# A hybrid decoder layer on one core: the copies into G turned, two diagonals, six row buffers, and the split of the transposed rows moved to the last groups of the G stage

## The chip, the core and the metric

The kernel runs on one core of one Trainium2 chip. The metric is the device time of one execution in microseconds (us). Several executions are timed, and their median is quoted. One execution was also profiled.

## The reference, cut to what matters

The layer works on 512 tokens of width 1024. A mixing sub-layer (sparse attention and a gated linear recurrence) ends in a layer norm. Behind it stands PEER, a retrieval over 128 x 128 = 16384 single-neuron experts:

```python
cand = s_top[:, :, 0, :, None] + s_top[:, :, 1, None, :]
cand_idx = i_top[:, :, 0, :, None] * 128 + i_top[:, :, 1, None, :]
best, pos = lax.top_k(cand.reshape(128, 8, 256), 16)
experts = jnp.take_along_axis(cand_idx.reshape(128, 8, 256), pos, axis=-1)
g = jax.nn.softmax(best, axis=-1)
h = jax.nn.gelu(jnp.einsum('td,thkd->thk', xb, u[experts]))
out = jnp.einsum('thk,thkd->td', g * h, v[experts])
```

Each token has 8 heads of 16 chosen experts, so 128 pairs (i, j), each with a gate weight. The last step is again a layer norm of ALPHA * h plus this sum.

## The kernel before

**Blocks.** The 512 tokens are four blocks of 128. Block 0 is mixed first, then blocks 1 to 3 together. For the retrieval, blocks 0 and 1 fetch the chosen rows of u and v by indirect DMA ("rows", one gather of 128 rows of 1024 numbers for each k of 128). Blocks 2 and 3 (`DENSE`) multiply with all 16384 experts instead, and a matrix G with the gate weight of every token at every expert picks the right ones.

**Rows.** `peer_gather` is a generator. Each step gathers rows on GpSimd's queue (L641) and lets VectorE work on them: the u rows are multiplied with the hidden state and summed (L665), the v rows are weighted and added (L678). Other code advances it by `pump`. Of block 0's v rows, the last 52 are not added by VectorE but by TensorE (`pe_gather`): ScalarE makes a diagonal `dg` from the identity and a gate column (L694), and TensorE multiplies it with the gathered rows (L696). The first 14 go to the tiles `pv` in the routing stage, 38 go to `pw`: `PEPRE` = 8 of them ahead of the G stage in the program, and 30 spread over its groups. There is one buffer for `dg`.

**Row buffers.** A gather writes in turn to four buffers of the pool tag `g` and to any buffer whose tag is in the list `lent`. Those are 128x1024 tiles that are not needed elsewhere for the moment. When the queries of blocks 1 to 3 are done, `lent` is cleared: `hx0`, `hx1`, `hs2` and `hs3` then take the transposed hidden state of blocks 2 and 3, split into a high part `hTh` (rounded, on ScalarE) and a low part `hTl` (the difference, on VectorE), 8 instructions in all (L893 and L894). From there to the end four buffers take rows.

**The G stage.** In `dense`, TensorE transposes indices and gates of blocks 2 and 3 (L725) and ScalarE copies them to `dtr` (L727). Then 64 groups of 4 tokens follow. For each, VectorE makes two one-hot tiles `og` of 128x512 (L749), and ScalarE multiplies the gate weight into the second of them, one token (128x128) an instruction (L753): 4 tokens in every other group, 3 in the rest, where VectorE does the fourth (L755). `GACTS` sets this. TensorE multiplies the two for each token (L758) into a PSUM tile `gb` of 4 x 128 (two buffers), and ScalarE copies that into G (L736, `evacuate`). G is laid out as expert row j, then token t, so the copy writes 128 numbers that lie 1024 bytes apart, for each of 4 tokens. In every third group the rows are pumped by one step.

**The dense stage.** For each of 128 j: hidden products with `hTh` and `hTl` (L785), GELU, weighting with `G[:, j, :]` (L791), and the sum into `acc` (L805). The rest of the rows of blocks 0 and 1 are pumped between.

**Order.** The Tile framework's scheduler orders each engine's instructions when the program is built, from a timing model of its own and the number of buffers of each tag. An engine then runs its list in order.

Of the kernel before, what the change touches and what calls it, by code (L numbers as in the profile page):

```python
# [9 lines left out]
F32 = mybir.dt.float32  # L10
F32R = mybir.dt.float32r
# [4 lines left out]
ALU = mybir.AluOpType  # L16
# [10 lines left out]
HGB = 5  # L27
GB = 4
UB = 4
VB = 3  # L30
HLB = 6
KB2 = 11
# [8 lines left out]
PEPRE = 8  # L41
PEG = 60

GACTS = (3, 4)

GPUMP = 3

# [4 lines left out]
def tile_decoder_layer(ctx, tc, a, out):  # L52
    nc = tc.nc

    cst = ctx.enter_context(tc.tile_pool(name="cst", bufs=1))
    gat = ctx.enter_context(tc.tile_pool(name="gat", bufs=5))
# [114 lines left out]
    hT_parts = {}  # L171
    lent = ["hs1", "hs2", "hs3", "hx0", "hx1"]
# [513 lines left out]
    def pe_gather(n, p):  # L686

        while 0 not in weighted:
            pump(1)
        ks = [pe_left.pop(0) for _ in range(n)]  # L690
        for k in ks:
            g = gather(a["v"], 0, k, "v")
            dg = gat.tile([128, 128], F32, name=f"dg{k}", tag="dg", bufs=1)
            nc.scalar.mul(dg, ident, gate[:, 0, k:k + 1])  # L694
            for i in range(2):
                nc.tensor.matmul(p[i], dg, g[:, i * 512:(i + 1) * 512], start=(k == ks[0]), stop=(k == ks[-1]))  # L696
            if k != ks[-1]:
                yield
        for i in range(2):
            y = hs[0][:, i * 512:(i + 1) * 512]  # L700
            nc.vector.tensor_tensor(y, y, p[i], op=ALU.add)
        yield
# [13 lines left out]
    def dense(den, dps):  # L716

        nb = len(DENSE)
        T = 128 * nb
        tr = {}  # L720
        hTh, hTl = hT_parts["h"], hT_parts["l"]
        for i, b in enumerate(DENSE):
            p = dps.tile([128, 512], F32, name=f"dtp{b}", tag="gb", bufs=2)
            for n, src in enumerate((keep[b][0], keep[b][1], gate[:, b, :])):
                nc.tensor.transpose(p[:, n * 128:(n + 1) * 128], src, ident)  # L725
            t = den.tile([128, 4, 128], F32, name=f"dtr{b}", tag="v", bufs=VB)
# [6 lines left out]
        G = den.tile([128, 128, T], F32, name="G")  # L733

        def evacuate(t0, p):
            nc.scalar.copy(G[:, :, t0:t0 + 4].rearrange("p j t -> p t j"), p)  # L736

        def pump_some(t0):
            if t0 // 4 % GPUMP == 0:
                pump(1)  # L740

        for t0 in range(0, T, 4):
            p = dps.tile([128, 4, 128], F32, name=f"gb{t0}", tag="gb", bufs=2)
            x = tr[DENSE[t0 // 128]]
            c = t0 % 128
            og = [den.tile([128, 4, 128], F32, name=f"og{t0}_{n}", tag=tag, bufs=bufs)
                  for n, (tag, bufs) in enumerate((("u", UB), ("hl", HLB)))]
            for n in range(2):
                nc.vector.tensor_tensor(og[n], iota[:, None, :].to_broadcast([128, 4, 128]),  # L749
                                        x[n][:, c:c + 4, None].to_broadcast([128, 4, 128]), op=ALU.is_equal)  # L750
            gact = GACTS[t0 // 4 % len(GACTS)]
            for tt in range(gact):
                nc.scalar.mul(og[1][:, tt, :], og[1][:, tt, :], x[2][:, c + tt:c + tt + 1])  # L753
            if gact < 4:
                nc.vector.tensor_tensor(og[1][:, gact:, :], og[1][:, gact:, :],  # L755
                                        x[2][:, c + gact:c + 4, None].to_broadcast([128, 4 - gact, 128]), op=ALU.mult)
            for tt in range(4):
                nc.tensor.matmul(p[:, tt, :], og[0][:, tt, :], og[1][:, tt, :], start=True, stop=True)  # L758
            if t0:
                evacuate(t0 - 4, last)  # L760
            last = p
            pump_some(t0)
            while pdone < PEK2 and pdone < PEPRE + (t0 // 4 + 1) * (PEK2 - PEPRE) // PEG:
                next(pw)
                pdone += 1
# [39 lines left out]
                    nc.tensor.matmul(acc[i][n], wt[:, sl], vt, start=(j == 0 and q == 0), stop=(j == 127 and q == 2))  # L805

        def residual():
            ia = gat.tile([128, 128], F32, name="ia", tag="dg", bufs=1)
            nc.scalar.mul(ia, ident, ALPHA)
            for i in range(nb):  # L810
                for n in range(2):
                    for c in range(4):
                        for t in (hTl, hTh):
                            nc.tensor.matmul(acc[i][n][:, c * 128:(c + 1) * 128],
                                             t[n].bitcast(F32)[:, c, i * 128:(i + 1) * 128], ia,
                                             start=False, stop=False)
# [29 lines left out]
    def stage(blocks, xT):  # L846
# [37 lines left out]
            for b in (1, 2):  # L884
                index["sc"][b] = choose(b, index["sc"][b])
        if blocks != [0]:
            lent.clear()
            for part, tags in (("h", ("hx0", "hx1")), ("l", ("hs2", "hs3"))):
                hT_parts[part] = [cst.tile([128, 4, 256], F32R, name=f"hT{part}{i}", tag=tag) for i, tag in enumerate(tags)]
            for k in range(0, 8, 2):  # L890
                x = hT[:, k:k + 2, 128:384]
                th, tl = [hT_parts[part][k // 4][:, k % 4:k % 4 + 2, :] for part in "hl"]
                nc.scalar.copy(th, x)  # L893
                nc.vector.tensor_tensor(tl, x, th.bitcast(F32), op=ALU.subtract)  # L894
            for _ in pe_gather(PEK1, [bank(f"pv{i}", "hg") for i in range(2)]):
                pass

# [57 lines left out]
```

## Time and profile before

| | |
|---|---|
| median of 3 runs | 1610.61 us (1610.09 to 1612.2) |
| profiled execution, its own time | 1619.35 us |
| its span, first to last instruction | 1617.6 us |
| TensorE busy | 1446.4 us, 89% of the span |
| VectorE busy | 1385.0 us, 86% |
| ScalarE busy | 707.1 us, 44% |
| GpSimd busy | 674.6 us, 42% |
| mean DMA rate | 289 GB/s |

The profile names TensorE PE (its weight loads PEld), VectorE DVE, ScalarE ACT, GpSimd POOL. Busy times are sums over stages that have different limits: the G stage and the dense stage follow one another, and ScalarE is busy in them to quite different degrees. The profiled execution is 8.7 us longer than the median of the timed runs, so a duration from the trace is a little on the long side for those.

### The profile page before, as it was taken

How to read it: one execution, taken by the hardware profiler on the slowest of the kernel's cores; microseconds unless marked ns; L12 is line 12 of the kernel's file. 1: busy time of each engine (PE TensorE's matmuls, PEld its weight loads, DVE VectorE, ACT ScalarE, POOL GpSimd, SP SyncE). 2: the span in 40 equal slices, each digit the busy share in tenths (PEclk: the TensorE clock that was granted, in tenths of full speed). 3: DMA queues.
4: the chain of work that ended last, by engine and by line, in shares of the span. 5: the costliest groups of instructions: out<-in, count | busy, mean ns of one | idle time of the engine just before them, and what ended most of it. 6: DMA issues, size and time to landing. Idle time of an engine off the chain costs nothing. (4 is left out here: it accounts for less than half of the span.)

```text
span 1617.6 us, 24516 instructions
## 1 busy us (share of the span) xinstructions
PE 1446.4 (89%) x7858; PEld 1090.0 (67%) x7858; DVE 1385.0 (86%) x3263; ACT 707.1 (44%) x1501; POOL 674.6 (42%) x531
## 2 busy tenths in 40 slices
PE   8997879755777799679989999999999999999996
PEld 4756534533443466236668888888888889989985
DVE  4219997888889889998887999899998999999998
ACT  3312121122332012249994555555555555555553
POOL 0000057757766440254443444444453346545440
PEclk9998989865789899999999999999999999999998
DMA  8454579989879871457678999999999999999995
GB/s 289 171 161 150 171 265 409 341 304 346 301 270 342 309 296 53 143 164 229 225 226 289 350 345 354 320 351 351 354 352 332 342 343 361 358 348 351 353 360 192
DMA packets 166162, 467.90 MB, mean 289 GB/s; under 512 B 18576, under 2 KB 18704, under 8 KB 165904
## 3 DMA queue, kind: packets, MB, share of 16 engines
q0 software_dynamic: 73728, 268.47, 47.4%
q1 hardware_dynamic: 92304, 197.86, 33.9%
q8 instruction: 62, 1.02, 0.2%
q14 instruction: 68, 0.56, 0.1%
HBM read 464.16 MB, written 2.10 MB: 288 GB/s over the span
## 5 line engine op out<-in xcount | busy, mean ns | idle before, releaser
L641 POOL DMA_INDIRECT gv<-in_v_dram,idx x256 | 340.8, 1331 | 400.4 <-DVE hs L678 237.5
L641 POOL DMA_INDIRECT gu<-in_u_dram,idx x256 | 323.0, 1262 | 433.3 <-DVE gu L665 193.0
L665 DVE SCALAR_TENSOR_TENSOR gu<-gu,hs 128x1024 f32<-128x1024 f32 x256 | 310.9, 1236 | 30.5 <-DMA gu<-in_u_dram,idx 30.0
L678 DVE SCALAR_TENSOR_TENSOR hs<-gv,gate,hs 128x1024 f32<-128x1024 f32 x204 | 261.5, 1282 | 12.1 <-DMA gv<-in_v_dram,idx 9.3
L774 ACT CAST v_0h<-v 128x512 fp32r<-128x512 f32 x128 | 79.7, 623 | 95.3 <-PE acc L805 57.9
L525 PE MATMUL pq<-hT,wpq 128*128 128x128 f32 (+1 forms) x512 | 118.4, 389 | 0.0
L774 ACT CAST v_1h<-v 128x512 fp32r<-128x512 f32 x128 | 79.5, 621 | 88.6 <-DMA v<-in_v_dram 40.2
L776 DVE TENSOR_TENSOR u_0l<-u,u_0h 128x512 fp32r<-128x512 f32 x128 | 88.5, 691 | 29.6 <-ACT u_0h L774 26.7
L774 ACT CAST u_0h<-u 128x512 fp32r<-128x512 f32 x128 | 79.3, 620 | 68.0 <-PE hp L785 32.1
L805 PE MATMUL acc<-v_0h,wl 128*128 128x512 f32 x256 | 102.0, 399 | 2.8 <-DVE wl L795 2.8
L776 DVE TENSOR_TENSOR v_1l<-v,v_1h 128x512 fp32r<-128x512 f32 x128 | 88.1, 688 | 17.2 <-ACT v_1h L774 13.9
L525 PEld LDWEIGHTS pq<-hT,wpq 128*128 128x128 f32 x512 | 79.9, 198 | 31.7 <-issue 1.1
L805 PE MATMUL acc<-v_0h,wh 128*128 128x512 f32 x256 | 101.2, 395 | 0.0
L774 ACT CAST u_1h<-u 128x512 fp32r<-128x512 f32 x128 | 79.4, 621 | 49.5 <-PE acc L805 42.1
L805 PE MATMUL acc<-v_1h,wl 128*128 128x512 f32 x256 | 100.3, 392 | 0.0
L805 PE MATMUL acc<-v_1h,wh 128*128 128x512 f32 x256 | 100.1, 391 | 0.0
L805 PE MATMUL acc<-v_0l,wh 128*128 128x512 f32 x256 | 99.7, 391 | 0.0
L776 DVE TENSOR_TENSOR u_1l<-u,u_1h 128x512 fp32r<-128x512 f32 x128 | 88.0, 687 | 5.8 <-ACT wh L793 2.3
L776 DVE TENSOR_TENSOR v_0l<-v,v_0h 128x512 fp32r<-128x512 f32 x128 | 88.2, 689 | 2.5 <-ACT v_0h L774 1.5
L785 PE MATMUL hp<-hTh,u_1l 128*128 128x256 f32 x512 | 84.8, 288 | 4.9 <-DVE u_1l L776 2.9
L785 PE MATMUL hp<-hTl,u_0h 128*128 128x256 f32 x512 | 83.8, 286 | 6.0 <-ACT u_0h L774 5.7
L785 PEld LDWEIGHTS hp<-hTl,u_0h 128*128 128x128 f32 x512 | 76.4, 189 | 18.6 <-ACT u_0h L774 8.8
(275 smaller groups left out, 3199.3 us busy)
## 6 DMA issues: line engine op xcount, KB each, us to landing
v<-in_v_dram SPq DMA_DIRECT2D x256, 256.0 KB
u<-in_ut_dram SPq DMA_DIRECT2D x256, 256.0 KB
wpq<-in_w_pq_dram SPq DMA_DIRECT2D x32, 512.0 KB
wo<-in_w_o_dram SPq DMA_DIRECT2D x16, 512.0 KB
hfw<-in_w_hf_dram SPq DMA_DIRECT2D x8, 512.0 KB
hqw<-in_w_hq_dram SPq DMA_DIRECT2D x8, 512.0 KB
hiw<-in_w_hi_dram SPq DMA_DIRECT2D x8, 512.0 KB
qaw<-in_w_qa_dram SPq DMA_DIRECT2D x8, 512.0 KB
```

Of the source, the lines that this page charges most:

```text
L525: nc.tensor.matmul(qp[:, :nt], w[:, k, :], hT[:, k, :nt], start=(k == 0), stop=(k == 7))
L641: nc.gpsimd.indirect_dma_start(out=t, out_offset=None, in_=table, in_offset=bass.IndirectOffsetOnAxis(ap=idx[b][k // 64][:, k % 64:k % 64 ...
L665: nc.vector.scalar_tensor_tensor(g, g, 1.0, hs[b], op0=ALU.mult, op1=ALU.mult, accum_out=hd[:, k:k + 1]))
L678: nc.vector.scalar_tensor_tensor(hs[b], g, gate[:, b, k:k + 1], hs[b], op0=ALU.mult, op1=ALU.add))
L774: nc.scalar.copy(h, x)
L776: nc.vector.tensor_tensor(l, x, h.bitcast(F32), op=ALU.subtract)
L785: nc.tensor.matmul(hp, ut[:, k * 128:(k + 1) * 128], ht[n][:, k, :], start=(n + q + k == 0), stop=(n == 1 and q == 2 and k == 3))
L805: nc.tensor.matmul(acc[i][n], wt[:, sl], vt, start=(j == 0 and q == 0), stop=(j == 127 and q == 2))
```

## The change

Four things are edited:

- **The copy into G is turned.** Source and target are walked in the other order: j outside, the 4 tokens inside. The writes now come in runs of 4 adjacent numbers (16 bytes), and the reads of PSUM jump 512 bytes from one number to the next.
- **`GACTS` is (4,)**: ScalarE does all four gate products in each group, VectorE none.
- **Two buffers for `dg`.**
- **`hs2` and `hs3` are lent to the rows**, so six buffers take rows from the routing stage on. In the place of the early split stand 4 plain copies to `hx0` and `hx1`. At group 56 (`t0 == T - 32`) the lending ends and the first half is split into `hs2` and `hs3`; at group 58 the second half is copied once more, into a row buffer of tag `g`, and split into `hx0` and `hx1`.

```diff
-GACTS = (3, 4)
+GACTS = (4,)
...
+DGB = 2
...
-            dg = gat.tile([128, 128], F32, name=f"dg{k}", tag="dg", bufs=1)
+            dg = gat.tile([128, 128], F32, name=f"dg{k}", tag="dg", bufs=DGB)
...
-            nc.scalar.copy(G[:, :, t0:t0 + 4].rearrange("p j t -> p t j"), p)
+            nc.scalar.copy(G[:, :, t0:t0 + 4], p.rearrange("p t j -> p j t"))
+
+        def split_hidden(x, h, l):
+            for k in (0, 2):
+                nc.scalar.copy(h[:, k:k + 2, :], x[:, k:k + 2, :])
+                nc.vector.tensor_tensor(l[:, k:k + 2, :], x[:, k:k + 2, :], h[:, k:k + 2, :].bitcast(F32), op=ALU.subtract)
...
+            if t0 == T - 32:
+                lent.clear()
+                x0, x1 = hT_parts["x"]
+                hTh, hTl = [[cst.tile([128, 4, 256], F32R, name=f"hT{part}0", tag=tag)]
+                            for part, tag in (("h", "hs2"), ("l", "hs3"))]
+                split_hidden(x0, hTh[0], hTl[0])
+            if t0 == T - 24:
+                x = gat.tile([128, 4, 256], F32, name="hTx1_moved", tag="g", bufs=GB)
+                nc.scalar.copy(x, x1)
+                for parts, part, tag in ((hTh, "h", "hx0"), (hTl, "l", "hx1")):
+                    parts.append(cst.tile([128, 4, 256], F32R, name=f"hT{part}1", tag=tag))
+                split_hidden(x, hTh[1], hTl[1])
...
-            lent.clear()
-            for part, tags in (("h", ("hx0", "hx1")), ("l", ("hs2", "hs3"))):
-                hT_parts[part] = [cst.tile([128, 4, 256], F32R, name=f"hT{part}{i}", tag=tag) for i, tag in enumerate(tags)]
+            lent[:] = ["hs2", "hs3"]
+            hT_parts["x"] = [cst.tile([128, 4, 256], F32, name=f"hTx{i}", tag=f"hx{i}") for i in range(2)]
             for k in range(0, 8, 2):
-                x = hT[:, k:k + 2, 128:384]
-                th, tl = [hT_parts[part][k // 4][:, k % 4:k % 4 + 2, :] for part in "hl"]
-                nc.scalar.copy(th, x)
-                nc.vector.tensor_tensor(tl, x, th.bitcast(F32), op=ALU.subtract)
+                nc.scalar.copy(hT_parts["x"][k // 4][:, k % 4:k % 4 + 2, :], hT[:, k:k + 2, 128:384])
```

The buffer counts also change the order that the scheduler makes. Three places follow, the kernel before first each time. The line numbers of the changed kernel are its own: its L697, L758 and L763 are L696, L753 and L758 before, and L736 is L736 in both.

On GpSimd's queue, where blocks 1 to 3 come out of their first layer norm, `gv_62` and so on are v rows of block 0 for VectorE, `gv_80` and `gv_81` are rows for the `pv` sums, which are due much later:

```order
210 L641 DMA gv_60_3460<-in_v_dram,idx_0_110 128x1024
211 L641 DMA gv_61_3463<-in_v_dram,idx_0_110 128x1024
212 L641 DMA gv_62_3466<-in_v_dram,idx_0_110 128x1024
213 L641 DMA gv_63_3485<-in_v_dram,idx_0_110 128x1024
214 L641 DMA gv_64_3488<-in_v_dram,idx_1_111 128x1024
```

```order
210 L642 DMA gv_60_3460<-in_v_dram,idx_0_110 128x1024
211 L642 DMA gv_61_3463<-in_v_dram,idx_0_110 128x1024
212 L642 DMA gv_80_4587<-in_v_dram,idx_1_111 128x1024
213 L642 DMA gv_81_4593<-in_v_dram,idx_1_111 128x1024
214 L642 DMA gv_62_3466<-in_v_dram,idx_0_110 128x1024
```

The two gathers that fill the newly lent `hs2` and `hs3` moved ahead of `gv_62`; they can start only when TensorE has transposed what those two buffers held.

On TensorE, at the end of routing: `dtp` are the transposes of indices (`ij`) and gates of the dense blocks, `pw` the products of the rows with a diagonal (`gv_90` is the first of them), `gb` the first groups of G:

```order
746 L725 MATMUL dtp_4669<-ident,ij_0_4114 128x128
747 L725 MATMUL dtp_4669<-ident,ij_1_4115 128x128
748 L725 MATMUL dtp_4669<-ident,gate 128x128
749 L696 MATMUL pw_4675<-gv_96_4713,dg_4715 128x512
750 L696 MATMUL pw_4676<-gv_96_4713,dg_4715 128x512
751 L696 MATMUL pw_4675<-gv_97_4719,dg_4721 128x512
752 L696 MATMUL pw_4676<-gv_97_4719,dg_4721 128x512
753 L758 MATMUL gb_4726<-og_1_4728,og_0_4727 128x128 x3
```

```order
750 L697 MATMUL pw_4669<-gv_98_4751,dg_4753 128x512
751 L697 MATMUL pw_4670<-gv_98_4751,dg_4753 128x512
752 L697 MATMUL pw_4669<-gv_99_4788,dg_4790 128x512
753 L697 MATMUL pw_4670<-gv_99_4788,dg_4790 128x512
754 L697 MATMUL pw_4669<-gv_100_4822,dg_4824 128x512
755 L697 MATMUL pw_4670<-gv_100_4822,dg_4824 128x512
756 L725 MATMUL dtp_4663<-ident,ij_0_4114 128x128
757 L725 MATMUL dtp_4663<-ident,ij_1_4115 128x128
758 L725 MATMUL dtp_4663<-ident,gate 128x128
759 L763 MATMUL gb_4720<-og_1_4722,og_0_4721 128x128 x4
```

The first `gb` stood behind 8 products of `pw` (`gv_90` to `gv_97`) and stands behind 11 now (to `gv_100`); all of these are ahead of the last transposes, where two followed them. On ScalarE, correspondingly, 13 of the 38 diagonals stand ahead of the copies to `dtr`, where 7 stood there before.

On ScalarE, near the end of the G stage of the changed kernel, the moved work among the groups (`hTx` is the kept copy, `hTh` the high part):

```order
440 L758 ACTIVATE og_1_5623<-og_1_5623,dtr_4667 128x128 x4
441 L758 ACTIVATE og_1_5637<-og_1_5637,dtr_4667 128x128 x4
442 L775 COPY hTx_moved<-hTx_4556 128x1024
443 L695 ACTIVATE dg_5810<-ident,gate 128x128
444 L736 COPY G<-gb_5550 128x128x4
445 L740 CAST hTh_5743<-hTx_4555 128x512 x2
446 L736 COPY G<-gb_5564 128x128x4
447 L758 ACTIVATE og_1_5660<-og_1_5660,dtr_4667 128x128 x4
448 L826 ACTIVATE ia<-ident 128x128
449 L758 ACTIVATE og_1_5674<-og_1_5674,dtr_4667 128x128 x4
450 L736 COPY G<-gb_5584 128x128x4
451 L740 CAST hTh_5788<-hTx_moved 128x512 x2
```

The copy to the row buffer and the two pairs of high parts are five instructions that ScalarE did not have in this stage before.

## Rows read from the trace of the kernel before

**Rows 1.** The page's first line.

```profile
span 1617.6 us, 24516 instructions
```

**Rows 2.** Windows: length, busy PE, PEld, DVE, ACT, POOL; clock, DMA share, GB/s.

```profile
590.00:620.00 30.00, 30.00 (x114) 19.10 (x113) 26.35 (x195) 5.81 (x12) 0.00 (x0) 1.00 0.41 143
620.00:655.00 35.00, 35.00 (x138) 22.42 (x137) 35.00 (x240) 10.98 (x19) 0.00 (x1) 1.00 0.03 10
655.00:713.00 58.00, 40.32 (x86) 14.38 (x84) 57.21 (x366) 15.50 (x33) 24.36 (x18) 0.94 0.51 155
713.50:849.00 135.50, 123.25 (x640) 84.01 (x638) 115.92 (x215) 130.36 (x322) 62.62 (x55) 0.99 0.71 228
849.00:1617.60 768.60, 741.48 (x4672) 666.50 (x4672) 701.87 (x1161) 399.44 (x775) 330.49 (x232) 0.99 0.94 337
```

**Rows 3.** Groups, 713 to 849 us: busy us, mean ns; idle us, releasers.

```profile
L749 DVE TENSOR_TENSOR og<-iota,dtr 128x512 f32<-128x512 f32 x128 | 81.1, 688 | 3.0 <-PE gb L758 2.2 <-ACT dtr L727 0.8
L753 ACT ACTIVATE og<-og,dtr 128x128 f32<-128x128 f32 x224 | 73.0, 412 | 0.0
...
L736 ACT COPY G<-gb 128x512 f32<-128x512 f32 x64 | 64.9, 1072 | 1.7 <-PE gb L758 1.7
...
L641 POOL DMA_INDIRECT gv<-in_v_dram,idx x31 | 37.9, 1223 | 25.3 <-PE pw L696 14.8 <-DVE gu L665 6.0 <-issue 3.0
...
L665 DVE SCALAR_TENSOR_TENSOR gu<-gu,hs 128x1024 f32<-128x1024 f32 x22 | 26.9, 1223 | 16.6 <-DMA gu<-in_u_dram,idx 16.6
...
L694 ACT ACTIVATE dg<-ident,gate 128x128 f32<-128x128 f32 x32 | 13.2, 412 | 5.5 <-PE pw L696 5.5
...
L755 DVE TENSOR_TENSOR og<-og,dtr 128x128 f32<-128x128 f32 x32 | 9.1, 285 | 0.2
```

**Rows 4.** ScalarE's timeline inside the G stage: start, length, instruction.

```profile
793.35 1.26 ACT L753 ACTIVATE og<-og,dtr 128x128 f32<-128x128 f32 x4
794.51 0.39 ACT L694 ACTIVATE dg<-ident,gate 128x128 f32<-128x128 f32 x1
...
795.68 1.94 ACT L736 COPY G<-gb 128x512 f32<-128x512 f32 x2
797.41 1.27 ACT L753 ACTIVATE og<-og,dtr 128x128 f32<-128x128 f32 x4
```

**Rows 5.** TensorE's timeline in the same stretch.

```profile
786.95 1.98 PE L696 MATMUL pw<-gv,dg 128*128 128x512 f32 x4 [0.33 <-ACT og L753]
788.77 2.00 PE L758 MATMUL gb<-og,og 128*128 128x128 f32 x16
790.95 1.98 PE L696 MATMUL pw<-gv,dg 128*128 128x512 f32 x4 [0.18 <-ACT dg L694]
```

**Rows 6.** ScalarE's timeline around the early split.

```profile
586.58 1.14 ACT L893 CAST hTh<-hT 128x512 fp32r<-128x512 f32 x2 [2.96 <-DVE hs L678]
...
590.40 1.57 ACT L534 COPY pss<-psc 128x512 f32<-128x512 f32 x3 [1.36 <-PE psc L529]
591.83 0.51 ACT L527 COPY pqs<-pq 128x384 f32<-128x384 f32 x1
```

**Rows 7.** VectorE's timeline at the same place.

```profile
587.74 2.49 DVE L894 TENSOR_TENSOR hTl<-hT,hTh 128x512 fp32r<-128x512 f32 x4
591.02 0.87 DVE L539 MAX8 sv<-pss 128x8 f32<-128x128 f32 x4 [0.79 <-ACT pss L534]
```

**Rows 8.** TensorE's timeline in the routing stage, the `pv` products.

```profile
657.75 1.98 PE L696 MATMUL pv<-gv,dg 128*128 128x512 f32 x4 [0.55 <-ACT dg L694]
660.29 1.98 PE L696 MATMUL pv<-gv,dg 128*128 128x512 f32 x4 [0.55 <-ACT dg L694]
...
687.45 3.77 PE L696 MATMUL pv<-gv,dg 128*128 128x512 f32 x4 [7.42 <-ACT dg L694]
```

**Rows 9.** All engines' timeline where `hs2` and `hs3` come free.

```profile
557.18 1.94 PE L213 MATMUL hT_ps<-ident,hs 128*128 128x128 f32 x8 [0.81 <-DVE hs L144]
...
558.50 1.86 POOL L641 DMA_INDIRECT gv<-in_v_dram,idx  x1 [14.04 <-DVE hs L678]
```

More of the change, by code (lines that the diff above doesn't have):

```diff
@@ L720, in dense @@
         tr = {}
-        hTh, hTl = hT_parts["h"], hT_parts["l"]
         for i, b in enumerate(DENSE):
@@ L807, in residual @@
         def residual():
-            ia = gat.tile([128, 128], F32, name="ia", tag="dg", bufs=1)
+            ia = gat.tile([128, 128], F32, name="ia", tag="dg", bufs=DGB)
             nc.scalar.mul(ia, ident, ALPHA)
```

## The prediction

> **What bounds the kernel now.** I read the stages first (busy time in windows), then the groups of the stage that the change touches, then its timeline engine by engine. In the windows [rows 2] the reader is to see three stages with three limits. From 590 to 655 us TensorE is busy all the time, and VectorE joins it at 620. From 655 to 713 VectorE is busy 57.2 of 58 us (routing), and TensorE only 40.3. Then comes the G stage, 713.5 to 849: ScalarE is busy 130.4 of 135.5 us, TensorE 123.3, VectorE 115.9. So ScalarE sets its pace, but TensorE stands only 7 us behind. Last comes the dense stage, 768.6 us, with TensorE at 741.5. No edit touches the work of that one: rows are pumped as often before it, and G has the same layout. The result is decided in the 135.5 us.
>
> The groups of the G stage [rows 3] show what fills ScalarE: 224 gate products, 64 copies into G, 32 diagonals. Their durations overlap, so I take what one occupies from the distance of starts in the timeline [rows 4]: four products from 793.35 to 794.51, 0.29 us each; a diagonal, of the same shape and the same mean of 412 ns [rows 3], as much; two copies into G from 795.68 to 797.41, 0.865 each. The check: 224 x 0.29 + 64 x 0.865 + 32 x 0.29 = 129.6, against 130.4 busy. TensorE in the same stretch [rows 5]: a product `pw` occupies 1.82 us (786.95 to 788.77), two groups of `gb` some 2.0, and its waits for ScalarE are only 0.2 to 0.3 us in a cycle of 4.0.
>
> **The change, part by part.**
>
> *The turned copy* is the large term, and no row shows it: nowhere in these rows does ScalarE read PSUM in jumps. Bounds: a copy of the same 512 numbers out of PSUM in plain order occupies 0.477 us (three from 590.40 to 591.83 [rows 6]); the present copy 0.865. I take 0.477, because the two differ only in the write order, and the new writes come in runs of four: 64 x 0.388 = 24.8 us less on ScalarE. The upper bound is no gain at all, 0.865.
>
> [...]
>
> *`GACTS` (4,)*: 32 more products on ScalarE, 32 x 0.29 = +9.3 us. VectorE loses 32 products of 0.285, at most 9.1 us [rows 3].
>
> *Diagonals and `pw`.* With two diagonals and six row buffers, the order puts 11 products `pw` ahead of the first group instead of 8, and 13 diagonals instead of 7 ahead of `dtr`. So the G stage loses 6 x 0.29 = 1.7 us on ScalarE and 3 x 1.82 = 5.5 us on TensorE. These products go to the routing stage. There a `pv` product starts every 2.53 us, 0.55 of it waiting for the single diagonal [rows 8]; with two it can be 1.98. From 655 to 713, 14 + 11 products take 25 x 1.98 = 49.5 us, and with the present wait of 7.42 for a gate column [rows 8] 56.9 of the 58 us. They just fit beside VectorE's work, which ends that stage; if they don't, the last transposes stand behind them on TensorE and G starts up to 2 us later. I count nothing for it.
>
> *The moved split.* In the G stage ScalarE gets four casts, 2 x 1.14 = 2.3 us, and one copy of 128x1024, priced as two of these, 1.1: +3.4 us. VectorE gets four subtractions, 2.5 us [rows 7]. Where they stood, four plain copies replace four casts on ScalarE (ScalarE is busy 5.8 of 30 us there [rows 2]), and VectorE loses 2.5 us at 588. I count that at nothing: VectorE then waits for TensorE's scores anyway (0.79 [rows 7], 3.65 us idle from 590 to 620), and TensorE is full until 655 [rows 2].
>
> *Six buffers on GpSimd's queue.* Two gathers into `hs2` and `hs3` now stand ahead of `gv_62`. They need the transposes that end at 559.1, while `gv_62` went out at 558.50 [rows 9]; each gather occupies the queue 1.2 us [rows 3], so what is behind it goes out 2 to 3 us later. VectorE's row additions then end that much later, and ScalarE's copies of the transposed rows wait for them (they wait 2.96 us now [rows 6]), with the `pss` copies behind them and VectorE's top-k behind these. The cover is the 2.5 us that VectorE no longer subtracts and its 3.65 idle until 620. So nothing; without the cover, 3 us. In the G stage six buffers let gathers go out earlier, and VectorE's wait of 16.6 us for u rows [rows 3] should shrink. Near its end the moved half holds one buffer; few gathers are left there.
>
> **The sum.** ScalarE: 130.4 - 24.8 + 9.3 - 1.7 + 3.4 = 116.6 us; with its present 5.1 idle, mostly at the start, 121.7. TensorE: 123.3 - 5.5 = 117.8; it can't lose its idle time at the start and at the end of the stage, some 5 us, so about 122.7. VectorE: 115.9 - 9.1 + 2.5 = 109.3 plus waits. Three engines then stand close together, TensorE and ScalarE handing two `gb` buffers to each other, so I add 1.3 us for waits that take turns: 124 us for the stage instead of 135.5, 11.5 us gained. The profiled execution took 1619.35 us, 1.75 more than its span of 1617.6 [rows 1], and would take 1607.9. It stands 8.7 us above the median of the runs, 1610.61, and I keep that distance: 1599.1 for the median.
>
> **The rivals.**
>
> *A: the price moves to the reading side (slower).* If the turned copy occupies 0.865 as before, ScalarE has 130.4 + 9.3 - 1.7 + 3.4 = 141.4 us, with 5.1 idle a stage of 146.5, 11 us longer: 1621.6. It decides at a copy of 0.693 us: 64 x 0.172 = 11.0 is what the other edits add to ScalarE. For it: no row has such a read, and the new pattern jumps 512 bytes at every number. Against it: the present copy, 0.865 against 0.477, reads in plain order and only writes in jumps, so the visible price is one of writing. One in five.
>
> *B: the rows become the bound.* ScalarE leaves the lead, but VectorE keeps its waits for u rows: 109.3 + 16.6 + 3.0 for groups and indices [rows 3] = 128.9 us, 6.6 gained, 1604.0. For it: TensorE and VectorE now take turns with GpSimd's single queue. Against it: six buffers. 15 in 100.
>
> *C: the edits cancel.* A copy between the bounds, about 0.69, gives ScalarE back just what the products and the split take from it, and the time stays within 0.2%. 8 in 100.
>
> **How the numbers follow.** The forecast has 55 in 100, rival B 15, C 8, A 20; 2 are left for a larger gain, up to the 18.9 us that a stage of ScalarE's 116.6 without idle time would give (1591.7). The forecast's own range is 1592 to 1606: from that lowest case to a stage that gains 4.6. The prediction is 1599.1. The range reaches from 1591 into the lower part of rival A, 1619; it leaves out most of A. A difference under 0.2% (3.2 us) is about what can't be told from no change here. Faster by more: forecast, B and the larger gain, 0.72. Within: C, 0.08. Slower: A, 0.20.
>
> **What would show it.** The row of the copy into G: near 0.6 us a piece (the plain copy's kind) in the forecast, near 1.07 in rival A. ScalarE in the G stage: no longer without any idle time, some 117 of 124 us, against 141 of 146. The number of `pw` products before the first `gb`: 11, and the first `og` still near 713; if it starts 2 us or more later, the cover in routing was too thin. VectorE's wait for u rows: under 5 us if the buffers help, 16 or more in rival B. The dense stage: 768 to 769 us as before; if that moves, the prediction is wrong in a place that it calls untouched.

## The result and the profile after

The changed kernel is slower: 1626.46 us, the median of 4 runs (1621.17 to 1627.2), against 1610.35 for the kernel before (1606.58 to 1612.2). The ratio is 1.0092, with a 95% interval of 1.0068 to 1.0115. The forecast was 1599.1 us, with a range of 1591 to 1619. Its profiled execution took 1627.2 us.

The page's first line and the windows of the changed kernel come first (length, busy PE, PEld, DVE, ACT, POOL; clock, DMA share, GB/s). The third window ends with VectorE's last index operation, the fourth with the first `og`, the fifth with the last `gb`.

```profile
span 1625.4 us, 24554 instructions
```

```profile
590.00:620.00 30.00, 30.00 (x118) 19.36 (x117) 29.96 (x231) 3.94 (x9) 0.00 (x0) 1.00 0.27 90
620.00:655.00 35.00, 35.00 (x126) 20.79 (x125) 35.00 (x219) 13.43 (x25) 6.52 (x5) 1.00 0.16 45
655.00:704.10 49.10, 30.72 (x69) 12.84 (x67) 49.03 (x324) 12.96 (x26) 25.18 (x14) 0.88 0.46 151
704.10:717.10 13.00, 7.93 (x15) 3.34 (x15) 0.03 (x1) 1.63 (x5) 6.60 (x8) 0.66 0.80 269
717.10:861.20 144.10, 120.85 (x630) 86.27 (x631) 113.31 (x195) 121.60 (x353) 51.22 (x48) 0.93 0.60 187
861.20:1625.40 764.20, 738.25 (x4665) 665.36 (x4663) 699.21 (x1153) 398.62 (x773) 328.39 (x230) 0.99 0.95 338
```

The reader is to see two things beside [rows 2]. For 13 us VectorE does nothing at all. And the G stage behind that is 144.1 us long, although no engine in it is full any more: ScalarE 121.6, TensorE 120.9, VectorE 113.3. The dense stage has not moved. The groups of the G stage (busy us, mean ns; idle us before, and releasers) say who waits:

```profile
L754 DVE TENSOR_TENSOR og<-iota,dtr 128x512 f32<-128x512 f32 x128 | 80.3, 684 | 41.2 <-PE gb L763 28.1 <-ACT dtr L727 13.0
...
L697 PE MATMUL pw<-gv,dg 128*128 128x512 f32 x120 | 64.4, 677 | 23.0 <-DMA gv<-in_v_dram,idx 22.3 <-ACT dg L695 0.6
...
L736 ACT COPY G<-gb 128x512 f32<-128x512 f32 x64 | 36.4, 577 | 10.5 <-PE gb L763 10.2
L666 DVE SCALAR_TENSOR_TENSOR gu<-gu,hs 128x1024 f32<-128x1024 f32 x23 | 28.0, 1216 | 0.0
```

Against [rows 3], the turned copy has a mean of 577 ns where it had 1072, and VectorE no longer waits for rows of u. In exchange TensorE waits 22.3 us for gathered rows of v, which stand in its list ahead of `gb`, and VectorE waits for TensorE and for `dtr`. One of TensorE's waits, 10.35 us, ends before the first `og` (below); from the first `og` to the last `gb` the table of waits (total us, times, longest) has

```profile
PE pw L697 <- DMA gv<-in_v_dram,idx: 12.0, 9, 2.9
```

**Where the time went.** I count from VectorE's last index operation, since executions differ ahead of it whatever the edit. The first transposes of `hT_ps` start at 552.70 us in the profile of before, and at 542.97 in that of the turned copy alone (below), though every engine's list is the same in both; after the change they start at 545.98, and over all kernels below between 542.97 and 559.67. From there to the last index it is 159.8 us before and 157.9 after, so that the edits cost nothing up to there. The last index comes at 712.49 before and at 703.90 after. From there to the first `hp` of the dense stage it is 137.1 us before (849.54) and 153.0 after (856.93): 16.0 us more, and the medians differ by 16.1. Of these, 12.2 are the later start (a wait of 13.00 for `dtr` in place of 0.76) and 9.6 the pace inside G (144.1 us from the first `og` to the last `gb`, 134.5 before); 5.8 come back at the end of G, where the first `hp` now stands 4.3 us ahead of the last `gb` and stood 1.5 behind it.

The start, in four timelines of the changed kernel (start, length, instruction, idle time before it): GpSimd, VectorE, TensorE, ScalarE.

```profile
691.18 1.36 POOL L642 DMA_INDIRECT gu<-in_u_dram,idx  x1 [0.30 <-PE pw L697]
692.84 11.60 POOL L642 DMA_INDIRECT gv<-in_v_dram,idx  x1 [0.30 <-PE pw L697]
704.74 0.94 POOL L642 DMA_INDIRECT gu<-in_u_dram,idx  x1 [0.30 <-issue]
```

```profile
703.90 0.22 DVE L623 SCALAR_TENSOR_TENSOR idx<-dc_v,dc_v 128x64 uint32<-128x64 f32 x1
717.12 1.29 DVE L754 TENSOR_TENSOR og<-iota,dtr 128x512 f32<-128x512 f32 x2 [13.00 <-ACT dtr L727]
```

```profile
683.91 12.26 PE L697 MATMUL pw<-gv,dg 128*128 128x512 f32 x28 [2.14 <-ACT gate L627]
...
708.57 7.60 PE L697 MATMUL pw<-gv,dg 128*128 128x512 f32 x12 [10.35 <-DMA gv<-in_v_dram,idx]
716.01 0.38 PE L725 MATMUL dtp<-ident,ij 128*128 128x128 f32 x2
```

```profile
716.27 0.40 ACT L695 ACTIVATE dg<-ident,gate 128x128 f32<-128x128 f32 x1 [1.31 <-PE pw L697]
716.58 0.84 ACT L727 COPY dtr<-dtp 128x384 f32<-128x384 f32 x2
...
734.45 1.04 ACT L736 COPY G<-gb 128x512 f32<-128x512 f32 x2
```

A gather that occupies GpSimd 0.94 us right behind it occupies it 11.60 here, until 0.3 us after VectorE's routing is done. TensorE's next `pw` product needs that row, and waits 10.35 us, to 4.1 us behind the gather's end. It is the first of three (a product is four matmuls), and the last transposes stand behind those, at 716.01. VectorE can't start G without them. (The last row, two copies into G, is for later.)

### The profile page after: what moved, and what is told of

The parts are those of the page before. It is cut to its first block, busy times and chain, and to the rows that moved or that the text cites. A ratio compares the mean times of both kernels' runs of the same rounds, so it can differ in the third digit from the quotient of the medians.

```text
span 1625.4 us, 24554 instructions
## 1 busy us (share of the span) xinstructions
PE 1444.4 (89%) x7858; PEld 1094.3 (67%) x7858; DVE 1376.8 (85%) x3231; ACT 699.1 (43%) x1538; POOL 681.6 (42%) x531
## 5 line engine op out<-in xcount | busy, mean ns | idle before, releaser
L642 POOL DMA_INDIRECT gv<-in_v_dram,idx x256 | 344.3, 1345 | 406.5 <-DVE hs L679 224.8
L642 POOL DMA_INDIRECT gu<-in_u_dram,idx x256 | 326.7, 1276 | 426.9 <-DVE gu L666 210.5
L754 DVE TENSOR_TENSOR og<-iota,dtr 128x512 f32<-128x512 f32 x128 | 80.3, 684 | 41.2 <-PE gb L763 28.1
L697 PE MATMUL pw<-gv,dg 128*128 128x512 f32 x152 | 78.5, 660 | 25.2 <-DMA gv<-in_v_dram,idx 22.3
```

Source lines behind the costliest of these rows:

```text
L642: nc.gpsimd.indirect_dma_start(out=t, out_offset=None, in_=table, in_offset=bass.IndirectOffsetOnAxis(ap=idx[b][k // 64][:, k % 64:k % 64 ...
```

## The experiments

The main theory was that the pieces work as forecast and the order around them loses the time: 11 products stand ahead of the last transposes, on rows that come late, and the gathers of v stand out of order on GpSimd. The rivals: an edit costs the time by itself (the turned read, the fourth product), or the six buffers do.

All ratios are to the kernel before on the same chip, with a 95% interval; 0.1% is 1.6 us. "G" is the profile's time from the start of the last index operation to the end of the last `gb`.

| kernel | `dg` buffers | row buffers | products on ScalarE | order kept | `pw` ahead | G, us | ratio (interval) |
|---|---|---|---|---|---|---|---|
| before (copy not turned) | 1 | 4 | 3, 4 | | 6 | 135.5 | 1 |
| changed | 2 | 6 | 4 | | 11 | 157.3 | 1.0092 (1.0068 to 1.0115) |
| turned copy alone | 1 | 4 | 3, 4 | | 6 | 131.1 | 0.9972 (0.995 to 0.9995) |
| with four products | 1 | 4 | 4 | | 6 | 144.0 | 1.0048 (1.0023 to 1.0072) |
| changed, one diagonal | 1 | 6 | 4 | | 3 | 137.7 | 1.0049 (1.0018 to 1.008) |
| changed, four rows | 2 | 4 | 4 | | 11 | 155.1 | 1.0146 (1.0093 to 1.0198) |
| products pinned | 2 | 6 | 4 | PE | 8 | 128.9 | 0.9963 (0.9943 to 0.9982) |
| gathers in order | 2 | 6 | 4 | POOL | 10 | 142.6 | 1.0032 (1.0011 to 1.0052) |
| both | 2 | 6 | 4 | PE, POOL | 8 | 124.9 | 0.9955 (0.9933 to 0.9978) |
| turned copy, six rows | 1 | 6 | 3, 4 | | 3 | 138.4 | 1.001 (0.9989 to 1.0032) |
| pinned, four rows | 2 | 4 | 4 | PE | 8 | 134.6 | 1.0011 (0.9981 to 1.004) |
| both, one diagonal | 1 | 6 | 4 | PE, POOL | 8 | 142.1 | 1.0081 (1.006 to 1.0103) |
| both, three and four products | 2 | 6 | 3, 4 | PE, POOL | 8 | 125.7 | 0.9953 (0.9928 to 0.9978) |
| four products, `og` pinned | 1 | 4 | 4 | DVE | 6 | 130.5 | 0.9958 (0.9937 to 0.998) |
| the same, u rows placed | 1 | 4 | 4 | DVE | 6 | 140.4 | 1.0026 (0.9997 to 1.0055) |

"`pw` ahead" counts the products ahead of the last transposes in TensorE's program order.

### The pieces one by one

**The turned copy alone.**

```diff
-            nc.scalar.copy(G[:, :, t0:t0 + 4].rearrange("p j t -> p t j"), p)
+            nc.scalar.copy(G[:, :, t0:t0 + 4], p.rearrange("p t j -> p j t"))
```

> The kernel before with the turned copy alone. Main theory (the 0.58 us copies seen after the change are a true gain, and the change loses elsewhere, at the late start of G and in its gathers): the order before G is that of the kernel before, 6 products of pw stand ahead of the last transposes, so VectorE's wait between routing and the first og stays under 2 us; ScalarE's busy time in G falls from 131 to about 103 us; G is then held by TensorE (120 us) and VectorE, and the time falls by 6 to 12 us, to 1598 to 1604 us. Rival 1 (the read at jumps of 512 bytes costs ScalarE or TensorE something that the copy's own row does not show): no gain, 1609 us or more.

0.9972: some 4.5 us faster, a little under the low end of what was expected. Every engine's list is that of before. The groups of its G stage:

```profile
L753 ACT ACTIVATE og<-og,dtr 128x128 f32<-128x128 f32 x224 | 72.1, 392 | 15.4 <-DVE og L749 15.4
...
L736 ACT COPY G<-gb 128x512 f32<-128x512 f32 x64 | 34.9, 571 | 2.1 <-PE gb L758 2.1
```

The copy is cheap, and ScalarE now waits 15.4 us for VectorE. VectorE in turn waits 14.6 us for rows of u, where it waited 16.6 [rows 3]. So the edit's own gain is real, rival A (and this study's rival 1) is out, and without ScalarE in the lead the rows hold the stage.

**Four products as well** (`GACTS` is (4,), nothing else).

> The turned copy and all four products on ScalarE, with four row buffers, one diagonal and the early split. Main theory: within 3 us of the run with the turned copy alone, VectorE's part of G shorter by about 9 us of busy time and ScalarE's longer by 9; 1597 to 1604 us. Rival 1 (the pieces themselves cost the time): 1612 us or more.

1.0048: 0.76% above the turned copy alone, some 12 us, where I had expected none. VectorE lost 9 us of work and the stage became 13 us longer. VectorE's wait for rows of u, in the table of waits (total us, times, longest), went from the first of these lines in the turned copy alone

```profile
DVE gu L665 <- DMA gu<-in_u_dram,idx: 14.6, 14, 3.0
```

to this one with four products:

```profile
DVE gu L665 <- DMA gu<-in_u_dram,idx: 29.5, 17, 3.3
```

TensorE's and GpSimd's lists are the same in both but for the first products in G. On VectorE the list changed: the rows of u stand behind groups 5, 5, 8, 10, 14, 16, 20, 22 in the one, and 1, 5, 8, 10, 12, 15, 19, 22 in the other. Two kernels further down take this up.

**The changed kernel with one diagonal** (`DGB` = 1) **and with four row buffers** (and the early split).

> The changed kernel with one diagonal instead of two; six row buffers and the late split stay. 3 products of pw now stand ahead of the last transposes instead of 11. Main theory: the wait for dtr between routing and G's first og falls from 13.0 us to under 2 us, and the time by 9 to 12 us, to 1614 to 1618 us; what stays above the turned copy alone is the pace of the gathers within G. Rival 2 (the six buffers, their order on GpSimd's queue, are the whole loss): it stays at 1623 to 1628 us with whatever wait.

> The turned copy, four products and two diagonals, with four row buffers and the early split. 11 products of pw stand ahead of the last transposes, as in the changed kernel, and the gathers stand in program order. Main theory: the first og comes 8 to 13 us after VectorE's last index operation, and the time is 8 to 12 us above the same kernel with one diagonal, 1607 to 1614 us. Rival 2 (the six buffers are the whole loss): within 2 us of the same kernel with one diagonal, 1597 to 1604 us.

With one diagonal the wait for `dtr` fell to 0.60 us, as expected, and the kernel is 0.43% faster than the changed one (the intervals overlap), 7 us of the 9 to 12 expected. G is 137.7 us; what it wins over the changed kernel it gives back in part behind G, where the span goes on for 778.6 us instead of 764.2. With four rows the late start is there with another set of buffers: 7.72 us of wait for `dtr`, and 0.98% (some 16 us, 8 to 12 expected) above the four-row kernel with one diagonal. So rival 2 is out: it is the two diagonals that bring the late start. The kernel lost more than that. In TensorE's list of before, one product stands behind every second group of G. In both kernels with two diagonals they stand unevenly (in the changed one in bunches, behind groups 8, 8, 10, 15, 15, 17, 21, 21, 23, 23, 25, 30, 30, in the four-row one behind 9, 9, 11, 13, 14, 17, 20, 21, 23, 26), and while TensorE waits for their rows the next groups wait behind them.

### The order put right

**The products pinned.** The 8 products are written ahead of the transposes, and TensorE keeps the order written:

```diff
-                nc.tensor.matmul(p[i], dg, g[:, i * 512:(i + 1) * 512], start=(k == ks[0]), stop=(k == ks[-1]))
+                tc.keep_in_program_order(
+                    nc.tensor.matmul(p[i], dg, g[:, i * 512:(i + 1) * 512], start=(k == ks[0]), stop=(k == ks[-1])))
...
+        pw = pe_gather(PEK2, [dps.tile([128, 512], F32, name=f"pw{n}", tag=f"acc0_{n}") for n in range(2)])
+        for _ in range(PEPRE):
+            next(pw)
+        pdone = PEPRE
...
-                nc.tensor.transpose(p[:, n * 128:(n + 1) * 128], src, ident)
+                tc.keep_in_program_order(nc.tensor.transpose(p[:, n * 128:(n + 1) * 128], src, ident))
```

> The changed kernel with 8 products of pw written ahead of the transposes, and the products and transposes of this stage kept in the order written on TensorE: 8 ahead of the last transposes instead of 11, then two products behind every second group of G. Main theory (G starts late since its transposes stand behind products that wait for a slow gather, and the four-row kernel with two diagonals lost 12 us so): VectorE's wait for dtr falls from 13.0 us to under 3 us and the time by 8 to 12 us, to 1614 to 1618 us. Rival (the fourth product on ScalarE is the loss, as 13 us between the two kernels with one diagonal and four rows would have it, and the start only moves the wait): the wait goes, the time stays above 1621 us.

0.9963, against 1.0092: 1.29% or some 21 us less than the changed kernel, twice what was expected, and all its edits are still in it. Its timelines of GpSimd and VectorE:

```profile
693.22 11.53 POOL L642 DMA_INDIRECT gv<-in_v_dram,idx  x1 [0.30 <-issue]
```

```profile
705.17 1.29 DVE L755 TENSOR_TENSOR og<-iota,dtr 128x512 f32<-128x512 f32 x2 [0.72 <-ACT dtr L732]
```

The slow gather is still there and as slow. But the product that needs it now stands behind the transposes, and nothing waits for it: 0.72 us for `dtr`. This settles the start, 12.3 us of the 21. The rest came inside G, where one product now stands behind every second group and TensorE waits for no row: it is 128.0 us from the first `og` to the last `gb`, 16 less than 144.1. Some 9 of these go again at its end, where the first `hp` stands 5.0 us behind the last `gb`.

**The gathers in order, and both together.** All row gathers are kept in program order on GpSimd; alone, and with the pinned products.

```diff
-        nc.gpsimd.indirect_dma_start(out=t, out_offset=None, in_=table,
-                                     in_offset=bass.IndirectOffsetOnAxis(ap=idx[b][k // 64][:, k % 64:k % 64 + 1], axis=0))
+        rows_in = nc.gpsimd.indirect_dma_start(
+            out=t, out_offset=None, in_=table,
+            in_offset=bass.IndirectOffsetOnAxis(ap=idx[b][k // 64][:, k % 64:k % 64 + 1], axis=0))
+        tc.keep_in_program_order(rows_in)
```

> The changed kernel with all row gathers kept on GpSimd's queue in the order in which the rows are used; 10 products of pw still stand ahead of the last transposes. Main theory: TensorE's wait for gathered rows within G (22 us in the changed kernel) falls under 10 us, the late start stays (5 us or more between the last index and the first og), and the time falls by 3 to 6 us, to 1620 to 1623 us. Rival (the order of the gathers is the whole loss): 1612 us or less.

> Both: 8 products pinned ahead of the transposes and the gathers in the order of use, with two diagonals, six row buffers, four products on ScalarE and the late split. Main theory: wait for dtr under 3 us, TensorE's wait for gathered rows in G under 8 us, G below 130 us from the first og, and 1600 to 1610 us. Rival (the fourth product on ScalarE is the loss): 1614 us or more, with VectorE waiting for rows of u.

Alone: 0.6% below the changed kernel, some 10 us, more than expected; 9.10 us of wait for `dtr` stay, and TensorE still waits 16.2 us for gathered rows from the last index on. Of these 7.8 are within G, where the changed kernel has 12.0; the 22 us of the expectation counted the wait at the start as well. Both: 0.9955, 1606.5 us against 1615.08 of the kernel before on that chip. The window from its first `og` to its last `gb`, and two of its groups:

```profile
706.60:830.70 124.10, 117.31 (x632) 81.00 (x632) 108.73 (x179) 117.98 (x354) 56.70 (x52) 0.97 0.70 230
```

```profile
L700 PE MATMUL pw<-gv,dg 128*128 128x512 f32 x120 | 57.5, 603 | 0.0
...
L739 ACT COPY G<-gb 128x512 f32<-128x512 f32 x64 | 35.2, 585 | 2.4 <-PE gb L766 2.4
```

TensorE waits for no row and no diagonal at all. A stage of the 124 us that the prediction worked out is here: 124.1 (134.5 before), with ScalarE at 118.0 (116.6 worked out), TensorE at 117.3 (117.8), VectorE at 108.7 (109.3). Whether the gathers' order adds to the pinned products can't be told: the intervals of 0.9963 and 0.9955 overlap, though G is 4 us shorter in the profile.

**The same with other buffers and products**, to see what each edit is worth where the order is even.

> The four-row kernel (turned copy, four products on ScalarE, two diagonals, early split) with 8 products pinned ahead of the transposes and two behind every second group, as in the pinned kernels with six rows; the gathers stand in the order of use. If the uneven order on TensorE was the loss there: the wait for dtr falls from 7.7 us to under 2 us and the time by 15 to 20 us, to about that of the kernel before plus or minus 4 us. What the pinned kernel with six rows has below it (it stood 0.45 per cent below the kernel before) is what the two rows more are worth: 3 to 10 us if VectorE's wait for rows of u (29.5 us with four rows and four products) is what they shorten, 0 if the rows were hidden.

> The kernel with pinned products and ordered gathers, with one diagonal instead of two. If two diagonals shorten TensorE's wait for dg (7 us in the kernel before, with one): 3 to 7 us slower than with two, with 5 us or more of PE waiting for dg. If the diagonal was hidden: within 2 us.

> The kernel with pinned products and ordered gathers, with three and four products on ScalarE in turn, as before the change. If the fourth product costs the time wherever it stands (13 us between the two kernels with four rows and one diagonal): 8 us or more faster than with four products. If that loss came from the order around it: within 3 us either way.

Pinned, the four-row kernel falls from 1.0146 to 1.0011, some 22 us, and its wait for `dtr` from 7.72 to 0.72 us: the order was its loss too. Six rows instead of four (and the late split with them) are worth 0.5% here (1.0011 against 0.9963 and 0.9955), some 8 us, as expected; VectorE waits 25.3 us for rows with four and 14.2 with six and the gathers in order. The fourth product makes no difference that can be told (0.9953 and 0.9955). The second diagonal is worth 1.3%, some 20 us, much more than expected. Inside G it is what was expected: with one diagonal TensorE waits 7.0 us for `dg`, and the stage is 129.9 us for 124.1 from the first `og` on. The larger part comes ahead of G. TensorE's timeline with one:

```profile
720.85 1.98 PE L700 MATMUL pw<-gv,dg 128*128 128x512 f32 x4 [0.55 <-ACT dg L697]
723.39 1.98 PE L700 MATMUL pw<-gv,dg 128*128 128x512 f32 x4 [0.55 <-ACT dg L697]
725.92 1.98 PE L700 MATMUL pw<-gv,dg 128*128 128x512 f32 x4 [0.55 <-ACT dg L697]
727.74 0.38 PE L732 MATMUL dtp<-ident,ij 128*128 128x128 f32 x2
```

With one diagonal a product starts every 2.53 us, the row of [rows 8]. The 8 that are pinned ahead of the transposes are then not done when the last index is (716.61), and VectorE waits 12.04 us for `dtr`. It is the changed kernel's loss again, made the other way round: the number of products ahead must fit the rate.

**The turned copy with six rows**, one diagonal, three and four products, and nothing pinned.

> The turned copy with six row buffers and the late split, but one diagonal and the products on ScalarE as before (3 and 4 in turn). The order on TensorE is the even one of the kernel before; the gathers stand out of order on GpSimd. If six buffers help where the order stays even: below the turned copy alone, 1598 to 1605 us. If the out-of-order gathers and the late split cost more than the buffers give: 1609 us or more.

1.001, 0.38% or 6 us above the turned copy alone (the intervals just meet): here the two buffers more, with the late split, bring nothing and rather cost time. GpSimd's list is out of order with six (v rows 101, 99, 100, then 105, 104, 106), and G is 138.4 us. As far as these kernels go, buffers pay only where the order of the gathers, or of their users, stays even.

### What four products changed on VectorE

The kernel with four products (four rows, one diagonal) again, with the `og` comparisons kept in the order written, so that a row of u stands behind every third group; and then with these rows placed behind the very groups where they stand in the turned copy alone.

```diff
-                nc.vector.tensor_tensor(og[n], iota[:, None, :].to_broadcast([128, 4, 128]),
-                                        x[n][:, c:c + 4, None].to_broadcast([128, 4, 128]), op=ALU.is_equal)
+                one = nc.vector.tensor_tensor(og[n], iota[:, None, :].to_broadcast([128, 4, 128]),
+                                              x[n][:, c:c + 4, None].to_broadcast([128, 4, 128]), op=ALU.is_equal)
+                tc.keep_in_program_order(one)
```

> The kernel with the turned copy and four products on ScalarE (four rows, one diagonal, early split), with the og comparisons kept in the order written on VectorE, so that a row of u is weighted behind every third group (1, 4, 7, 10, ...). Without this it took 13 us more than the turned copy alone, with VectorE waiting 29.5 us for rows of u instead of 14.6. If the place of the u rows between the groups made that loss: 6 to 13 us less than without it, and VectorE's wait for rows below 20 us. If the fourth product on ScalarE made it: no change within 3 us.

> The same, with the rows of u weighted behind the very groups behind which they stand in the kernel with the turned copy alone (5, 5, 8, 10, 14, 16, 20, 22, ...: two and four groups apart in turn). If the place of the u rows made the loss: within 3 us of the turned copy alone, 0.3 per cent below the kernel before, and G near 131 us from the last index. If the fourth product made it: it stays near 0.5 per cent above the kernel before, and G near 144 us.

Evenly spaced: 0.9958, 0.9% or some 14 us below the same kernel without it, and not to be told from the best above, with four rows, one diagonal and the early split. Its wait for rows:

```profile
DVE gu L665 <- DMA gu<-in_u_dram,idx: 9.3, 8, 1.6
```

So the fourth product did not make the loss; the order did. The second kernel missed what I expected of it: 1.0026, G 140.4, 19.1 us of wait. The same groups do not give the same time; its products of v stand one group later on TensorE than in the turned copy alone. What exactly is good about that kernel's order stays open.

### The slow gather

The one-hot work of the routing in f32 instead of bf16, in two halves (`io16`, the codes, `tab` and `oh`), and nothing else.

```diff
-            tab = pj(f"tab{b}_{z}_{half}").bitcast(BF).rearrange("p (h c k) -> p h c k", h=4, c=16)
...
+            for q in range(2):
+                Q = slice(half * 4 + 2 * q, half * 4 + 2 * q + 2)
+                tab = pj(f"tab{b}_{z}_{half}_{q}").rearrange("p (h c k) -> p h c k", h=2, c=16)
```

> The changed kernel with the one-hot work of the routing in f32 on VectorE, in two halves, and nothing else changed; VectorE's routing gets 10 to 25 us longer by itself, so the time is not the question. If VectorE's bf16 operations hold up GpSimd's gathers (11.60 and 3.01 us in the changed kernel, ending as these operations end): the gathers in that stretch take 0.9 to 1.6 us, and the first og follows the last index within 3 us. If something else holds them (the tables, the DMA rings): gathers of 3 us or more stay.

The time is beside the question (1.0202, since VectorE's routing is longer). No gather between 690 us and the first `og` takes more than 1.41 us, and the first `og` follows 0.95 us behind the last index. GpSimd's last gathers there:

```profile
711.97 0.94 POOL L644 DMA_INDIRECT gu<-in_u_dram,idx  x1 [1.36 <-DMA gv<-in_v_dram,idx]
714.24 1.41 POOL L644 DMA_INDIRECT gv<-in_v_dram,idx  x1 [1.33 <-PE pw L699]
716.35 1.29 POOL L644 DMA_INDIRECT gv<-in_v_dram,idx  x1 [0.70 <-PE pw L699]
```

But only the last two fall into the f32 one-hot work, which starts at 713.38 in this block and ends at 741; the others went out ahead of it, and the next one follows at 744.64. In the kernel with both orders kept the bf16 work of this block starts at 689.74, and the gathers at the same place in it are as short; its slow one, of 11.53 us, comes behind them at 694.75:

```profile
691.28 1.23 POOL L642 DMA_INDIRECT gv<-in_v_dram,idx  x1 [0.78 <-DVE dc_m L596]
693.00 1.45 POOL L642 DMA_INDIRECT gu<-in_u_dram,idx  x1 [0.49 <-PE pw L700]
```

So the expected rows came, but this run does not show that f32 work leaves gathers alone: where the slow gather stands it issued none.

## Why the prediction was wrong, point by point

**What bounds the kernel now**: right. ScalarE held the G stage, and a cheaper copy alone made it 4.4 us shorter (135.5 to 131.1). That TensorE stood close behind was right as well; that rows of u stood there too was the weight of rival B.

**The turned copy**: right. Two copies in a row take 1.04 us, at a mean of 577 ns for one, so that one occupies some 0.47 us (1.04 - 0.577), where 0.477 was estimated from the plain copy of [rows 6]. Rival A and rival C, which hung on it, are out.

**`GACTS`, the diagonals' cost, the moved split, the sum**: right in size where the order is even. 124.1 us for the stage against 124 worked out, with each engine within 1.4 us of its sum. That is a check of the whole and not of each term, and in part luck: the sum has 11 products ahead of the stage, that kernel has 8. The moved split's five instructions on ScalarE take 3.3 us in the changed kernel (3.4 worked out). And by the timed runs that kernel is 0.45%, some 7 us, below the kernel before, where the forecast had 11.5; where the rest goes, no run here shows.

**Diagonals and `pw`: this step failed.** It said of the 25 products: "They just fit beside VectorE's work, which ends that stage; if they don't, the last transposes stand behind them on TensorE and G starts up to 2 us later. I count nothing for it." The mechanism was named, but its price was 12.2 us, not 2. I made the sum for TensorE alone, as though its rows were there. For TensorE alone it was on the safe side: 7 products take 12.26 us in the changed kernel, 1.75 each, where I took 1.98. But the products ahead need rows, GpSimd issues these, and one gather took 11.60 us. The profile of before shows the same kind in the same stretch, and I had not read it. Its GpSimd, VectorE and TensorE:

```profile
702.65 3.16 POOL L641 DMA_INDIRECT gv<-in_v_dram,idx  x1 [1.60 <-PE pw L696]
...
708.05 4.95 POOL L641 DMA_INDIRECT gv<-in_v_dram,idx  x1 [0.30 <-DVE oh L616]
```

```profile
712.49 0.23 DVE L622 SCALAR_TENSOR_TENSOR idx<-dc_v,dc_v 128x64 uint32<-128x64 f32 x1
```

```profile
717.06 2.45 PE L696 MATMUL pw<-gv,dg 128*128 128x512 f32 x4 [2.00 <-DMA gv<-in_v_dram,idx]
```

The second gather ends 0.3 us behind VectorE's last index, and TensorE starts on its row 4.1 us later. There the row belonged to a product behind the transposes, so that the first `og` did not wait for it, and TensorE only 2.00 us. With that product and two more ahead of the transposes, an estimate from these rows would have been 0.3 + 4.1 + 3 x 1.82 us, and some 1.1 from the last transposes to the first `og` (716.01 to 717.12 above): 11 us between the last index and the first `og`, where 13.00 were measured.

**The order inside the G stage: left out.** I read the new order at its start and took the rest as before. With two diagonals the scheduler also bunched the products inside G, 27 here, and with six buffers it mixed the gathers. TensorE then waits 12.0 us for rows within G, VectorE 28.1 for `gb`, and the stage is 144.1 us from its first `og` instead of 124. The addition of 1.3 us "for waits that take turns" was the term for this, and it was 20 us too small: of the 27 us between the forecast and the result this step is the larger, the start has 12, and some 6 came back at the end of G. Pinning the products alone takes back the start and most of this, 21 us in all.

**Six buffers**: the harm feared at `gv_62` did not come (157.9 us from the first `hT_ps` to the last index, 159.8 before). The gain came only in the pinned kernels, some 8 us. Rival B, "the rows become the bound", was nearest of the rivals in kind: rows do hold G, though as rows of v on TensorE and not of u on VectorE, and to the other side.

**The dense stage**: untouched, as said (764.2 us from the last `gb` on, ahead of which it had already worked 4.3; 769.4 in the kernel with both orders kept, 769.6 before).

## What to carry to other kernels

A buffer count is an edit of the order. Where a scheduler decides, compare the whole of each engine's list around the change, and pin the order first: here the same edits cost 0.9% with the order left free and gained 0.45% with it pinned. Before moving products ahead of something that everything waits for, price the slowest arrival of their inputs in that very stretch (11.60 us for one gather here), not their own time (1.75 us for a product). When the leading engine is relieved, look for the ring behind it (row used, buffer free, gather, row used); its length depended here on where in the lists its members stood (VectorE's wait for rows of u was 29.5 us with four products and 9.3 with `og` pinned as well).

## What the hardware showed unexpectedly

**A slow gather ends with VectorE's routing work.** In the rows above a gather mostly occupies GpSimd 0.93 to 1.5 us. At the end of routing one takes 4.17 to 11.60 us in 11 of the 14 kernels whose timelines of GpSimd and VectorE stand side by side here, and in all 11 it ends 0.28 to 0.32 us behind VectorE's last index operation (704.44 against 704.12 in the changed one, 713.00 against 712.72 before). One of the other three is the f32 kernel above, which issued none there. In another, the changed one with four rows, VectorE had one gap in that work, 0.86 us for a table. These are VectorE's and GpSimd's timelines there:

```profile
697.28 0.69 DVE L616 TENSOR_TENSOR oh<-oh,tab 128x1024 bf16<-128x1024 bf16 x1
698.83 0.69 DVE L616 TENSOR_TENSOR oh<-oh,tab 128x1024 bf16<-128x1024 bf16 x1 [0.86 <-ACT tab L612]
```

```profile
693.03 5.75 POOL L641 DMA_INDIRECT gu<-in_u_dram,idx  x1 [1.70 <-PE pw L696]
```

The gather ended at 698.78, inside the gap. That the stalls come from VectorE's work is an inference from these ends, which no run shows: none takes the work away. Nor does every gather there end with a pause of VectorE: the next two gathers there (1.25 us at 699.09 and 1.10 at 700.64) ended while VectorE worked on, as did these in the third kernel, the pinned one with four rows, where VectorE has no gap from 696 to 712:

```profile
702.95 2.30 POOL L641 DMA_INDIRECT gu<-in_u_dram,idx  x1 [0.30 <-issue]
705.55 1.63 POOL L641 DMA_INDIRECT gv<-in_v_dram,idx  x1 [0.30 <-issue]
```

In the changed kernel the gather of 11.60 us, with one of 0.94 right behind it, lies over many of VectorE's instructions, none longer than 0.68 us. Which of them hold it, if any do, the rows don't show: casts and scalar operations, of 0.18 to 0.22 us, stand between the bf16 comparisons in that stretch.

**ScalarE's copies that read PSUM in jumps of 512 bytes took no longer than plain ones**: means of 571 (the turned copy alone, and with four products), 577 (the changed kernel) and 585 ns (both orders kept) for 128x512, against 1072 for the copy that wrote in jumps of 1024 bytes and a median of 586 for the plain copy to `pss` (L534) in the kernel before.

**TensorE's clock**: TensorE stood idle from 698.2 us on, waiting for the gather; the granted clock, 1.00 up to 702.0, was 0.50 from 702.8 on and back at 1.00 at 713.0:

```profile
702.80:713.00 10.20, 4.43 (x6) 1.80 (x7) 1.26 (x8) 0.40 (x1) 5.79 (x6) 0.50 0.76 275
```

The three products that G waited for began at 0.50 and took 7.4 us (708.57 to 716.01); seven of those ahead of them took 12.26 us at 1.00, 5.3 for three. In the G stage with its waits the clock is 0.93 in the mean, where the kernel before had 0.99. A `pw` matmul has a mean of 677 ns there, and of 603 in the kernel with both orders kept, at 0.97.
